# Gate matrices of a 16384-expert layer: outer products on TensorE for three token blocks, or indirect accumulating DMA into DRAM tables for two of them

## The chip, the cores and the metric

The kernel runs on one core of one Trainium2 chip. The metric is the device time of one execution in microseconds (us), less is better. Of the kernel before three timed runs are shown and one profiled execution. TensorE (PE in the profile) multiplies; VectorE (DVE) and ScalarE (ACT) do elementwise work; GpSimd (POOL) here mostly issues DMAs whose addresses come from a table of indices; SyncE (SP) issues nearly all other DMAs.

## What is computed

Two blocks of a network run one behind the other on 512 tokens of width 1024. The change is in the last layer of the second, a mixture of 16384 experts of one row each. Cut to what matters:

```
q = x @ wq                                   # 8 heads, two halves of 128 per head
scores = q . sub_keys                        # 128 scores per half
s_top, i_top = top_k(scores, 16)             # both halves
best_s, best_pos = top_k(all 16*16 sums, 16) # per head
expert = i_top[0]*128 + i_top[1]             # 8*16 = 128 experts per token
gate = softmax(best_s)                       # 128 gates per token
act = gelu(x . u_tab[expert]) * gate
out = sum(act * v_tab[expert])               # then a layer norm
```

## The kernel before

The first 2350 us or so are two layers of feed-forward and token mixing and the second block's token mixing; the change leaves them alone but for one place. What follows is `peer()`.

The 512 tokens are four blocks of 128. **Block 0** takes the reference's way: `chosen()` fetches for each of the 128 expert slots one row of `u_tab`, later one of `v_tab`, for all its 128 tokens by an indirect DMA on POOL's queue (L1737), and DVE multiplies the row (L1721) or adds it up (L1729), three gathers behind the issue; 256 such gathers in all. **Blocks 1 to 3** (384 tokens) are done densely: for each of 128 *columns* j (a column is the 128 experts with first index j) `proj` multiplies all 384 tokens with the column's 128 rows of `u_tab` (24 matmuls, L283, in three groups of eight: high by high, low by high, high by low part), the result goes through Gelu and is multiplied with a matrix of gates that is zero wherever a token did not choose the expert; then the column's rows of `v_tab` are multiplied in (18 matmuls, L1822) and accumulate over all columns. So each column needs a 128 by 384 slab of gates, `G[:, :, j]`.

`route()` finds experts and gates. It is a generator, and each `next()` is a *step*. In four *quads* (four score matrices each, after four units of `wq`) DVE takes the top 16 of each score matrix and of the sums; `resolve` turns positions into indices and softmaxes the gates. Then for six half blocks of 64 tokens (`BLOCKS`) it builds the gate slab: four tokens a step get two one-hot matrices on DVE (`o1` L1679, `o2` L1681), the second scaled by the gate on ACT (`og` L1683), four outer products on TensorE (`gp` L1690), and a copy out on ACT (`st` L1691). A finished half block is written to a DRAM tensor `G` ("gates", L1704); the last stays in SBUF.

The columns pass in three stages.

- **Kept stage.** While routing is unfinished, a column's activation (`hg`, L1839) is written to DRAM (`HS`, "acts"). The loop runs `routed(ROUTE_STEPS)` (2.3 steps of routing a column) and `gather(...)` (1.2, later 0.8 gathers a column) beside each column. It takes 92 columns: `kept` is 92.
- **Fused stage.** The other 36 columns need no store: activation (`hs`), gate, `v_tab` matmuls, with 2.6 gathers a column.
- **Tail.** The 92 kept columns are read back (`hs` from `acts`, `gq` from `gates`, L1876 and L1878) and take their `v_tab` matmuls, one gather a column. The layer norms of the four blocks end the program.

Each weight unit of 512 KB is loaded by SP, its high part is taken on ACT (`wh` L260) and its low part on DVE (`wl` L261); three such pairs and four raw buffers exist. A scheduler orders the instructions of each engine; each engine then runs its own list strictly in that order.

The loop of the kept stage reads:

```
        while not over or kept % 2:
            g = self.t32("hg")[:, GT:]
            activations(kept, g)
            nc.scalar.dma_start(HS[kept], g)
            over = over or routed(ROUTE_STEPS)
            gather(ROW_STEPS[self.known == P])
            kept += 1
```

Of the kernel before, what the change touches and what calls it, by code (L numbers as in the profile page):

```python
# [19 lines left out]
P = 128  # L20
S = 512
# [16 lines left out]

GT = 128
BT = 64  # L40
BLOCKS = [(t, a, a + BT) for t in range(NT) for a in range(0, P, BT) if t * P + a >= GT]

# [4 lines left out]

ROUTE_STEPS = 2.3
ROW_STEPS = (1.2, 0.8, 2.6, 1.0)

# [143 lines left out]
class Net:  # L194
    def __init__(self, tc, A, es):
# [8 lines left out]
        self.phase = es.enter_context(ExitStack())  # L204
        self.evn = 0

        c = self.const
# [320 lines left out]
    def ada_steps(self, l, n):  # L528
# [16 lines left out]
        if kind == 2 and i != 1:  # L545
            nc.vector.tensor_scalar(m, m, 0.5, None, op0=OP.mult)
        yield

    def fill(self, n):
# [1048 lines left out]
    def route(self, X, G, begun):  # L1598
# [3 lines left out]
        best, pos, itop, numbers, iis = {}, {}, {}, {}, {0: self.ii0}  # L1602
        for quad in range(4):
            keys = self.blk(name="keys")
            nc.sync.dma_start(keys, self.A["keys"][:, quad * 4:(quad + 1) * 4].rearrange("p a b -> p (a b)"))
# [6 lines left out]
            for t in range(NT):  # L1612
# [27 lines left out]
                if t == 0:  # L1640
# [6 lines left out]
                    nc.vector.tensor_copy(self.experts[:, q], e)  # L1647
                    self.known += 32
                elif t == BLOCKS[0][0] and quad == 3:
                    iis[t] = self.blk(name="ii")  # L1650
                    yield from self.resolve(best[t], pos[t], itop[t], iis[t], 0, 8)
        for n, (t, a, b) in enumerate(BLOCKS):
            for v in (t, BLOCKS[n + 1][0] if n + 1 < len(BLOCKS) else t):
# [46 lines left out]
            if n == len(BLOCKS) - 1:  # L1700
                self.last_gates = st
            else:
                for q in range(4):
                    nc.sync.dma_start(G[:, n, q * 32:(q + 1) * 32], st[:, q * 32:(q + 1) * 32])  # L1704
                yield
# [40 lines left out]
    def peer(self, out, begun):  # L1746
# [5 lines left out]
        self.pools(blocks, 22, {"A": 3, "S": 1, "T": 4})  # L1752
        n, last, early = S - GT, len(BLOCKS) - 1, GT // P
        G = self.dram.tile([P, last, NE, BT], F32, name="gates")
        HS = self.dram.tile([NE, P, n], F32, name="acts")
# [5 lines left out]
        ln = cst[:, 384:400].rearrange("p (a b) -> p a b", a=2)  # L1761
        nc.gpsimd.dma_start(ln, A["ln"])
        c0 = stage.tile([P, S], F32, name="c0", tag="c0")
        self.ii0, self.gates0, self.experts = c0[:, :256], c0[:, 256:384], c0[:, 384:].bitcast(I32)
# [27 lines left out]

        def routed(steps):
            nonlocal pace
            pace += steps
            while pace >= 1.0:
                pace -= 1.0
                with self.tc.issue_after(self.latest):
                    if next(work, self) is self:
                        return True  # L1800
            return False
# [27 lines left out]

        def gates(tile, j):  # L1830

            g4 = tile.rearrange("p (b i t) -> p b i t", i=2, t=BT)
            nc.sync.dma_start(g4[:, :last], G[:, :, j:j + 2])
            nc.scalar.activation(g4[:, last], self.last_gates[:, j:j + 2], AF.Copy)
            return g4

# [4 lines left out]
        kept, over = 0, False  # L1841
        while not over or kept % 2:
            g = self.t32("hg")[:, GT:]
            activations(kept, g)
            nc.scalar.dma_start(HS[kept], g)
            over = over or routed(ROUTE_STEPS)
            gather(ROW_STEPS[self.known == P])
            kept += 1
        self.kept = kept
        acc += [self.bank("acc", t) for t in "TTTTSA"]  # L1850
        fused, g4 = [], None
        for j in range(kept, NE):
            if j % 2 == 0:
                g4 = gates(stage.tile([P, 2 * n], F32, name="gs", tag="gs"), j)
            hs = self.blk(name="hs")[:, :n]
            activations(j, hs)
            nc.vector.tensor_mul(hs.rearrange("p (b t) -> p b t", t=BT), hs.rearrange("p (b t) -> p b t", t=BT),
                                 g4[:, :, j % 2])
            hi, lo = (v[:, :n] for v in self.new_pair())
            self.split(hs, hi, lo)  # L1860
            fused.append((*self.unit(A["pv"][:, j]), hi, lo))
            gather(ROW_STEPS[2])
            if len(fused) > 1:
                both(fused.pop(0))
# [8 lines left out]
        def fetch(j):  # L1873
            if j < kept:
                hs, g = self.blk(name="hs")[:, :n], self.blk(name="gq")[:, :n]
                nc.sync.dma_start(hs, HS[j])  # L1876
                g3 = g.rearrange("p (b t) -> p b t", t=BT)
                nc.sync.dma_start(g3[:, :last], G[:, :, j])  # L1878
                nc.scalar.activation(g3[:, last], self.last_gates[:, j], AF.Copy)
                coming.append((hs, g))  # L1880
# [44 lines left out]
        for j in range(kept - ENDS):  # L1925
            both(weighted(j) if j else first)
            if not self.gathered:
                gather(ROW_STEPS[3])
                if self.gathered:
# [12 lines left out]
def program(tc, A, out):  # L1942
    with ExitStack() as es:
# [21 lines left out]
        for l in range(DEPTH):  # L1965
            begun = net.ffn(l, 0, begun, lambda: to_mix(l))
            begun = net.mix(l, begun, lambda: to_ffn(l, 1))
            if l + 1 < DEPTH:
                net.side = side(l + 1, (1, 0, 2, 3, 4, 5, 6, 7, 8))
            begun = net.ffn(l, 1, begun, lambda: to_ffn(l + 1, 0) if l + 1 < DEPTH else to_second())  # L1970
        net.peer(out, net.mix2(begun))
# [17 lines left out]
```

## Time and profile before

| what | value |
|---|---|
| median of three timed runs | 3681.9 us (3677.95 to 3684.1) |
| profiled execution, its own time | 3671.99 us |
| its span | 3670.2 us |
| mean granted TensorE clock | 0.988 |
| columns kept / fused | 92 / 36 |

The span is the time from the first to the last instruction of the profiled execution. TensorE is busy for 97% of it, so a stage is best read by how many matmuls it runs and how long it lasts.

### The profile page before, as it was taken

The page shows a single profiled execution, that of the slowest core. Times are in us where ns is not written, and L with a number is a line of the kernel's source. Part 1 is how long each engine was busy: PE and PEld are TensorE (multiplying, and loading weights), DVE is VectorE, ACT ScalarE, POOL GpSimd, SP SyncE. Part 2 cuts the span into 40 slices and gives each one's busy share as a digit, 9 for nine tenths or more (in the row PEclk, how much of TensorE's full clock was granted, in tenths as well). Part 3 has the DMA queues.
Part 4 walks back from the last instruction along what each step waited for, and adds up shares of the span by engine and source line. Part 5 has one row for each costly group of instructions (what it writes and reads, how often), then busy time and mean ns, then how long its engine had stood idle before and what let it go on. Part 6 is the DMA issues. An engine that isn't in the chain of part 4 may idle for free. (4 is left out here: it accounts for less than half of the span.)

```text
span 3670.2 us, 49271 instructions
## 1 busy us (share of the span) xinstructions
PE 3554.5 (97%) x18265; PEld 3019.0 (82%) x18265; DVE 2394.7 (65%) x4791; ACT 1562.9 (43%) x2769; POOL 369.2 (10%) x358
## 2 busy tenths in 40 slices
PE   7999999999999999999999999899899999999998
PEld 6888876788888888767888887788899999988786
DVE  6555687665563334776533386699877667778787
ACT  4332366433233323465432263433667753334333
POOL 0000100000000001000000000021221134432220
PEclk9999999999999999999999999999999999999999
DMA  7666320266653333401333322265686879999995
GB/s 249 190 186 198 115 94 18 64 202 193 201 178 109 94 95 105 133 24 31 91 98 93 97 79 68 84 202 195 206 289 235 296 262 308 313 327 346 336 341 183
DMA packets 259665, 635.72 MB, mean 173 GB/s; under 512 B 82336, under 2 KB 117584, under 8 KB 256864
## 3 DMA queue, kind: packets, MB, share of 16 engines
q1 hardware_dynamic: 206368, 473.96, 40.1%
q0 software_dynamic: 39808, 140.52, 11.2%
q10 hardware_dynamic: 13248, 18.09, 1.3%
q8 instruction: 143, 2.34, 0.3%
q14 instruction: 98, 0.80, 0.1%
HBM read 591.32 MB, written 41.16 MB: 172 GB/s over the span
## 5 line engine op out<-in xcount | busy, mean ns | idle before, releaser
L260 ACT ACTIVATE wh<-raw 128x1024 fp32r<-128x1024 f32 (+2 forms) x620 | 645.3, 1043 | 1129.3 <-PE proj L283 880.6
L261 DVE TENSOR_TENSOR wl<-raw,wh 128x1024 fp32r<-128x1024 f32 (+2 forms) x620 | 744.1, 1201 | 508.4 <-ACT wh L260 370.1
L283 PE MATMUL proj<-yh,wh 128*128 128x512 f32 (+1 forms) x2744 | 644.7, 375 | 9.1 <-ACT hg L1839 4.2
L283 PE MATMUL proj<-yh,wl 128*128 128x512 f32 (+1 forms) x2744 | 629.1, 371 | 13.6 <-DVE wl L261 13.6
L283 PE MATMUL proj<-yl,wh 128*128 128x512 f32 (+1 forms) x2744 | 628.4, 370 | 0.0
L283 PEld LDWEIGHTS proj<-yh,wl 128*128 128x128 f32 x2744 | 506.4, 189 | 82.8 <-DVE wl L261 15.5
L283 PEld LDWEIGHTS proj<-yh,wh 128*128 128x128 f32 x2744 | 501.1, 189 | 85.0 <-ACT hg L1839 5.7
L283 PEld LDWEIGHTS proj<-yl,wh 128*128 128x128 f32 x2744 | 505.4, 189 | 67.5
L535 DVE SCALAR_TENSOR_TENSOR scr<-raw,cact 128x1024 bf16<-128x1024 f32 x128 | 156.7, 1224 | 136.3 <-DMA raw<-in_wada 136.0
L1822 PE MATMUL acc<-wl,yh 128*128 128x512 f32 x756 | 236.2, 394 | 2.7 <-DVE wl L261 2.6
L1822 PE MATMUL acc<-wh,yh 128*128 128x512 f32 x756 | 235.0, 392 | 3.6 <-ACT yh L266 2.1
L1822 PE MATMUL acc<-wh,yl 128*128 128x512 f32 x756 | 234.3, 391 | 0.3 <-DVE yl L267 0.3
L1737 POOL DMA_INDIRECT row<-in_purows,c x128 | 156.5, 1223 | 537.9 <-DVE row L1721 261.6
L667 DVE TENSOR_TENSOR ga<-sg,proj 128x512 f32<-128x512 f32 x88 | 60.5, 687 | 225.7 <-PE proj L283 223.2
L1737 POOL DMA_INDIRECT row<-in_pv,c x128 | 165.2, 1291 | 392.6 <-DVE vacc L1729 275.8
L272 PE MATMUL proj<-yl,wh 128*128 128x256 f32 (+1 forms) x552 | 177.0, 330 | 10.6 <-DVE yl L394 7.0
L273 PE MATMUL proj<-yh,wl 128*128 128x256 f32 (+1 forms) x552 | 174.6, 324 | 2.2 <-DVE wl L261 2.2
L1822 PEld LDWEIGHTS acc<-wl,yh 128*128 128x128 f32 x756 | 141.1, 188 | 38.4 <-DVE wl L261 9.5
L271 PE MATMUL proj<-yh,wh 128*128 128x256 f32 (+1 forms) x552 | 164.8, 328 | 7.8 <-ACT yh L640 6.3
L1822 PEld LDWEIGHTS acc<-wh,yh 128*128 128x128 f32 x756 | 142.1, 189 | 32.0 <-ACT yh L266 2.5
L1822 PEld LDWEIGHTS acc<-wh,yl 128*128 128x128 f32 x756 | 142.5, 189 | 31.4 <-DVE yl L267 1.0
L1729 DVE SCALAR_TENSOR_TENSOR vacc<-row,act,vacc 128x1024 f32<-128x1024 f32 x127 | 162.5, 1280 | 0.6
(465 smaller groups left out, 5166.7 us busy)
## 6 DMA issues: line engine op xcount, KB each, us to landing
raw<-in_wada SPq DMA_DIRECT2D x144, 512.0 KB
raw<-in_pu SPq DMA_DIRECT2D x128, 512.0 KB
raw<-in_pv SPq DMA_DIRECT2D x128, 512.0 KB
raw<-in_wg SPq DMA_DIRECT2D x84, 512.0 KB
raw<-in_wu SPq DMA_DIRECT2D x84, 512.0 KB
raw<-in_wd SPq DMA_DIRECT2D x64, 512.0 KB
gates<-st SPq DMA_DIRECT2D x20, 1024.0 KB
acts<-hg ACTq DMA_DIRECT2D x92, 192.0 KB
```

Source lines behind the costliest of these rows:

```text
L260: nc.scalar.activation(h[:, :n], raw[:, :n], AF.Copy)
L261: self.latest = nc.vector.tensor_sub(l[:, :n], raw[:, :n], h[:, :n].bitcast(F32)).ins
L271: mm(out, lhsT=lh, rhs=rh, start=start, stop=False)
L272: mm(out, lhsT=lh, rhs=rl, start=False, stop=False)
L273: mm(out, lhsT=ll, rhs=rh, start=False, stop=stop)
L283: self.nc.tensor.matmul(ps, lhsT=w[:, k * P:(k + 1) * P], rhs=X[c + k][part], start=c + k + i == 0, stop=i == 2 and c + k == nk - 1)
L535: nc.vector.scalar_tensor_tensor(scr, raw, 1.0, self.cact, op0=OP.mult, op1=OP.mult, accum_out=self.mod[:, l, j:j + 1])
L667: nc.vector.tensor_mul(a, sg, p[1])
L1729: nc.vector.scalar_tensor_tensor(acc, row, a, acc, op0=OP.mult, op1=OP.add)
L1737: nc.gpsimd.indirect_dma_start(out=row, out_offset=None, in_=tables[kind], in_offset=bass.IndirectOffsetOnAxis(ap=self.experts[:GT, s:s + ...
L1822: nc.tensor.matmul(acc[q], lhsT=a[:, t * P:(t + 1) * P], rhs=half(w, m), start=q not in started, stop=end and i == 2)
```

## The change

Gates of token blocks 1 and 2 are no longer built by outer products. Two DRAM tables of 16384 by 128 numbers (8 MB each, `table1`, `table2`) are set to zero during the last feed-forward of the first network, by 32 DMAs of 512 KB on POOL's queue. In each quad `resolve` now also runs for blocks 1 and 2 (two heads at a time, as for block 0), an index `expert*128 + token` is computed, and `spread_gates` issues for each of 128 slots and both tables one indirect DMA with add: 128 gates, one from each partition, four bytes each, to 128 places of the table (L1837). Only block 3 keeps its outer products (2 half blocks in place of 6). Routing now takes 2.3 steps a column in the first quad, 1.0 in the others and 1.8 behind them; 1.3 slots a column are spread; gathers go at 0.9 a column in the kept stage. The stage also lasts until all slots are issued: the built program keeps 110 columns (110 DMAs to `acts`) and fuses 18. A column's gates are now read by three DMAs (two tables and `G`) in place of one.

```
+TABLES = (1, 2)
-BLOCKS = [(t, a, a + BT) for t in range(NT) for a in range(0, P, BT) if t * P + a >= GT]
+BLOCKS = [(NT - 1, a, a + BT) for a in range(0, P, BT)]
-ROUTE_STEPS = 2.3
-ROW_STEPS = (1.2, 0.8, 2.6, 1.0)
+ROUTE_STEPS = (2.3, 1.0, 1.8)
+TABLE_STEPS = 1.3
+ROW_STEPS = (0.9, 2.6, 1.0)
...
+    def clear_tables(self):
+        nc = self.nc
+        for T in self.tables:
+            for q in range(NE // 8):
+                if q % 4 == 0:
+                    z = self.t32("zero")
+                    nc.gpsimd.memset(z, 0.0)
+                out = T[q * 8 * P * P:(q + 1) * 8 * P * P].rearrange("(p a c) o -> p a (c o)", p=P, a=2)
+                with self.tc.issue_after(self.latest):
+                    nc.gpsimd.dma_start(out, z[:, None, :].to_broadcast([P, 2, S]))
+                yield
...
+                elif t in TABLES:
+                    ii, q, n = self.blk(name="ii"), quad * 32, TABLES.index(t)
+                    yield from self.resolve(best[t], pos[t], itop[t], ii, quad * 2, 2)
+                    e, idx = self.sm(32, "enum"), self.idx[:, n * P + q:n * P + q + 32]
+                    nc.vector.scalar_tensor_tensor(e, ii[:, P + q:P + q + 32], float(NE), ii[:, q:q + 32],
+                                                   op0=OP.mult, op1=OP.add)
+                    nc.vector.tensor_scalar(e, e, float(P), self.pid, op0=OP.mult, op1=OP.add)
+                    nc.vector.tensor_copy(idx, e)
+                    self.ready[n] += [(idx[:, i:i + 1], best[t][:, q + i:q + i + 1]) for i in range(32)]
...
+        def spread_gates(columns):
+            nonlocal share
+            share = min(share + columns, 2.0)
+            while share >= 1.0 and all(self.ready):
+                share -= 1.0
+                for T, r in zip(self.tables, self.ready):
+                    idx, g = r.pop(0)
+                    with self.tc.issue_after(self.latest):
+                        nc.gpsimd.indirect_dma_start(out=T, out_offset=bass.IndirectOffsetOnAxis(ap=idx, axis=0), in_=g,
+                                                     in_offset=None, compute_op=OP.add)
...
-        def gates(tile, j):
-            g4 = tile.rearrange("p (b i t) -> p b i t", i=2, t=BT)
-            nc.sync.dma_start(g4[:, :last], G[:, :, j:j + 2])
...
+        def gates(tile, j, m):
+            g3 = tile.rearrange("p (i t) -> p i t", i=m)
+            for i, T in enumerate(self.tables):
+                nc.sync.dma_start(g3[:, :, i * P:(i + 1) * P],
+                                  T[j * P * P:(j + m) * P * P].rearrange("(i p t) o -> p i (t o)", p=P, t=P))
+            nc.sync.dma_start(g3[:, :, n - 2 * BT:n - BT], G[:, j:j + m])
+            nc.scalar.activation(g3[:, :, n - BT:], self.last_gates[:, j:j + m], AF.Copy)
...
-        while not over or kept % 2:
+        while not over or kept % 2 or self.ready[0]:
...
-            over = over or routed(ROUTE_STEPS)
-            gather(ROW_STEPS[self.known == P])
+            over = over or routed()
+            spread_gates(TABLE_STEPS)
+            gather(ROW_STEPS[0])
...
+            else:
+                net.side = net.clear_tables()
```

On POOL's queue, in the kept stage, there stood only gathers of block 0 (`row` from `in_purows`), each waiting for DVE to free a row buffer:

```order
L1737 DMA row<-in_purows,c_19132 128x1024 [waits DMASW4_49,DVE_49]
L1737 DMA row<-in_purows,c_19132 128x1024 [waits DMASW5_49,DVE_49]
L1737 DMA row<-in_purows,c_19132 128x1024 [waits DMASW6_49,DVE_49]
L1737 DMA row<-in_purows,c_19132 128x1024 [waits DMASW7_49,DVE_49]
L1737 DMA row<-in_purows,c_19132 128x1024 [waits DMASW0_49,DVE_49]
```

In the same stage of the changed kernel the two tables (`table_72` and `table_73`) alternate between the gathers; DMASWn are the semaphores of POOL's own earlier DMAs, used in turn:

```order
L1837 DMA table_73<-x_91,idx 2097152x1 [waits DMASW6_49,DVE_49,Activation_49]
L1837 DMA table_72<-x_90,idx 2097152x1 [waits DMASW5_49]
L1837 DMA table_73<-x_91,idx 2097152x1 [waits DMASW6_49]
L1837 DMA table_72<-x_90,idx 2097152x1 [waits DMASW7_49]
L1837 DMA table_73<-x_91,idx 2097152x1 [waits DMASW0_49]
L1837 DMA table_72<-x_90,idx 2097152x1 [waits DMASW1_49]
L1837 DMA table_73<-x_91,idx 2097152x1 [waits DMASW2_49]
L1766 DMA row<-in_purows,c_19184 128x1024 [waits DVE_49]
L1837 DMA table_72<-x_90,idx 2097152x1 [waits DMASW3_49]
```

Each of these waits names the semaphore of the previous DMA to the same table, two places up, so a scatter is issued only when the one before it to its table has landed. Between the first and the last scatter stand 256 scatters and 73 gathers; in 54 places the next scatter goes to the same table as the last. The first of them stand ahead of the gather whose row DVE takes at column 15, the last behind that of column 95.

On TensorE, in the later part of the kept stage, outer products (`gp`) stood between the columns' matmuls:

```order
L283 MATMUL proj<-yh,wl 128x384 x8
L283 MATMUL proj<-yl,wh 128x384 x8
L283 MATMUL proj<-yh,wh 128x384 x2
L1690 MATMUL gp<-og,o_23913 128x128 x3
L283 MATMUL proj<-yh,wh 128x384
L1690 MATMUL gp<-og,o_23913 128x128
L1690 MATMUL gp<-og,o_23922 128x128
```

In the changed kernel most of the stage holds columns and now and then the score matmuls of a quad (`sc`):

```order
L288 MATMUL proj<-yh,wh 128x384 x8
L288 MATMUL proj<-yl,wh 128x384 x8
L288 MATMUL proj<-yh,wl 128x384 x8
L1639 MATMUL sc<-keys,x_93 128x128
L1639 MATMUL sc<-keys,x_94 128x128
L1639 MATMUL sc<-keys,x_95 128x128
L1639 MATMUL sc<-keys,x_96 128x128
```

The outer products went from 384 to 128 and now stand only near the end of the stage.

On SP's queue, in the tail, a column had three DMAs:

```order
L1876 DMA hs<-acts 128x384
L1878 DMA gq<-gates 128x5x64
L257 DMA raw<-in_pv 128x1024
L1876 DMA hs<-acts 128x384
L1878 DMA gq<-gates 128x5x64
```

Now it has five:

```order
L1926 DMA hs<-acts 128x384
L1881 DMA gq<-table_72 128x128
L1881 DMA gq<-table_73 128x128
L1883 DMA gq<-gates 128x64
L262 DMA raw<-in_pv 128x1024
```

The bytes of a column's gates are the same; they come from three tensors.

## Rows read from the trace of the kernel before

**Rows 1.** The page, its part 1: busy time by engine.
```profile
PE 3554.5 (97%) x18265; PEld 3019.0 (82%) x18265; DVE 2394.7 (65%) x4791; ACT 1562.9 (43%) x2769; POOL 369.2 (10%) x358
```

**Rows 2.** Writers of the activations: ns min/median/max of one, first and last start.
```profile
L1839 ACT ACTIVATE hg<-proj x92: 463/490/500, 2365.8 to 2966.1; 128x384 f32<-128x384 f32 x92
...
L1839 ACT ACTIVATE hs<-proj x36: 473/492/492, 2970.3 to 3256.9; 128x384 f32<-128x384 f32 x36
```

**Rows 3.** Busy times of the engines in four stretches, with granted clock and DMA.
```profile
core 0: us, PE busy (x) PEld busy (x) DVE busy (x) ACT busy (x) POOL busy (x), PEclk, DMA share, GB/s
1600.00:2100.00 500.00, 490.32 (x2456) 397.34 (x2456) 232.43 (x444) 194.74 (x356) 2.08 (x4) 0.99 0.25 75
...
2445.00:2608.00 163.00, 146.38 (x736) 134.96 (x735) 150.96 (x676) 54.05 (x71) 22.39 (x20) 0.92 0.53 172
2608.00:2966.00 358.00, 345.34 (x2225) 341.55 (x2224) 267.57 (x440) 263.70 (x612) 74.18 (x55) 1.00 0.76 264
...
3257.00:3630.00 373.00, 368.25 (x1591) 298.86 (x1590) 298.55 (x400) 147.14 (x278) 88.68 (x85) 0.99 0.99 333
```

**Rows 4.** Timeline of TensorE: start and length in us, then the instructions.
```profile
2705.28 1.63 PE L283 MATMUL proj<-yh,wh 128*128 128x384 f32 x8
...
2709.52 1.95 PE L1690 MATMUL gp<-og,o 128*128 128x128 f32 x16
2711.23 0.94 PE L283 MATMUL proj<-yh,wh 128*128 128x384 f32 x4
```

**Rows 5.** Timeline of TensorE earlier in the kept stage.
```profile
2457.49 0.84 PE L283 MATMUL proj<-yl,wh 128*128 128x512 f32 x3
2462.61 2.93 PE L283 MATMUL proj<-yh,wl 128*128 128x384 f32 x8 [4.28 <-DVE wl L261]
...
2471.51 1.98 PE L283 MATMUL proj<-yh,wh 128*128 128x512 f32 x8
...
2476.95 1.98 PE L283 MATMUL proj<-yh,wh 128*128 128x512 f32 x8
...
2482.39 0.83 PE L1620 MATMUL sc<-keys,x 128*128 128x128 f32 x6
```

**Rows 6.** Groups by line and shape, 2366 to 2966: busy us, mean ns, idle before.
```profile
L261 DVE TENSOR_TENSOR wl<-raw,wh 128x1024 fp32r<-128x1024 f32 x104 | 126.7, 1222 | 76.8 <-ACT wh L260 69.4 <-PE proj L283 6.6 <-issue 0.8
...
L1690 PE MATMUL gp<-og,o 128*128 128x128 f32 x768 | 100.8, 279 | 9.4 <-ACT og L1683 8.7 <-ACT st L1691 0.8
...
L1679 DVE TENSOR_TENSOR o<-pcst,tr 128x512 f32<-128x512 f32 x96 | 65.5, 687 | 11.8 <-PE gp L1690 11.7
...
L1729 DVE SCALAR_TENSOR_TENSOR vacc<-row,act,vacc 128x1024 f32<-128x1024 f32 x29 | 37.1, 1279 | 0.1
L1681 DVE TENSOR_TENSOR o<-iota,tr 128x512 bf16<-128x512 bf16 x96 | 37.0, 421 | 9.8 <-issue 5.5 <-DMA acts<-hg 4.3
```

**Rows 7.** Timeline of POOL where gathers stand back to back.
```profile
2388.93 1.01 POOL L1737 DMA_INDIRECT row<-in_purows,c  x1 [61.56 <-DVE pcst L1551]
2390.24 0.99 POOL L1737 DMA_INDIRECT row<-in_purows,c  x1 [0.30 <-issue]
2391.54 0.93 POOL L1737 DMA_INDIRECT row<-in_purows,c  x1 [0.30 <-issue]
```

**Rows 8.** Timeline at the program's start: a DMA's issue and its first user.
```profile
0.76 0.39 SPq L509 DMA_DIRECT2D x<-in_x  x1
...
1.28 0.72 POOL L210 DMA_DIRECT2D ident<-in_ident  x1 [0.82 <-POOLq L1980]
...
3.57 0.63 ACT L605 ACTIVATE sq<-x 128x512 f32<-128x512 f32 x1 [1.53 <-DMA x<-in_x]
...
6.07 0.23 DVE L214 CAST identb<-ident 128x128 bf16<-128x128 f32 x1 [4.68 <-DMA ident<-in_ident]
```

**Rows 9.** The tail's gate reads by tile: ns of one issue on SP.
```profile
L1878 SPq DMA_DIRECT2D gq<-gates x92: 523/524/721, 3259.1 to 3607.6; - x92
```

**Rows 10.** Groups by line and shape, 3257 to 3630: who waits for the gates.
```profile
L1891 DVE TENSOR_TENSOR hs<-hs,gq 128x384 f32<-128x384 f32 x92 | 50.7, 557 | 69.6 <-DMA gq<-gates 67.5 <-ACT gq L1879 1.9
```

More of the change, by code (lines that the diff above doesn't have):

```diff
@@ L205, in __init__ @@
         self.evn = 0
+        self.tables = [self.dram.tile([NE * NE * P, 1], F32, name=f"table{t}") for t in TABLES]
         c = self.const
@@ L1603, in route @@
         for quad in range(4):
+            self.part = min(quad, 1)
             keys = self.blk(name="keys")
@@ L1651, in route @@
                     yield from self.resolve(best[t], pos[t], itop[t], iis[t], 0, 8)
+        self.part = 2
         for n, (t, a, b) in enumerate(BLOCKS):
@@ L1703, in route @@
                 for q in range(4):
-                    nc.sync.dma_start(G[:, n, q * 32:(q + 1) * 32], st[:, q * 32:(q + 1) * 32])
+                    nc.sync.dma_start(G[:, q * 32:(q + 1) * 32], st[:, q * 32:(q + 1) * 32])
                 yield
@@ L1752, in peer @@
         self.pools(blocks, 22, {"A": 3, "S": 1, "T": 4})
-        n, last, early = S - GT, len(BLOCKS) - 1, GT // P
-        G = self.dram.tile([P, last, NE, BT], F32, name="gates")
+        n, early = S - GT, GT // P
+        G = self.dram.tile([P, NE, BT], F32, name="gates")
         HS = self.dram.tile([NE, P, n], F32, name="acts")
@@ L1762, in peer @@
         nc.gpsimd.dma_start(ln, A["ln"])
+        self.pid = cst[:, 400:401]
+        src = A["iota"]
+        nc.gpsimd.dma_start(self.pid, bass.AP(tensor=src.tensor, offset=src.offset, ap=[[1, P], [1, 1]]))
+        self.idx = stage.tile([P, 2 * P], I32, name="idx", tag="idx")
+        self.ready, self.part = [[] for _ in TABLES], 0
         c0 = stage.tile([P, S], F32, name="c0", tag="c0")
@@ L1791, in gather, with routed @@
                     credit = credit - 1.0 if next(rows, False) else 0.0
-        def routed(steps):
+        share = 0.0
+        def spread_gates(columns):
[8 more added lines that the diff above has]
+                                                     in_offset=None, compute_op=OP.add)
+        def routed():
             nonlocal pace
-            pace += steps
+            pace += ROUTE_STEPS[self.part]
             while pace >= 1.0:
@@ L1828, in both @@
                 second(*args, end, t)
-        def gates(tile, j):
-            g4 = tile.rearrange("p (b i t) -> p b i t", i=2, t=BT)
-            nc.sync.dma_start(g4[:, :last], G[:, :, j:j + 2])
-            nc.scalar.activation(g4[:, last], self.last_gates[:, j:j + 2], AF.Copy)
-            return g4
+        def gates(tile, j, m):
[5 more added lines that the diff above has]
+            nc.scalar.activation(g3[:, :, n - BT:], self.last_gates[:, j:j + m], AF.Copy)
+            return g3
         def activations(j, g):
@@ L1850, in peer @@
         acc += [self.bank("acc", t) for t in "TTTTSA"]
-        fused, g4 = [], None
+        fused, g3 = [], None
         for j in range(kept, NE):
             if j % 2 == 0:
-                g4 = gates(stage.tile([P, 2 * n], F32, name="gs", tag="gs"), j)
+                g3 = gates(stage.tile([P, 2 * n], F32, name="gs", tag="gs"), j, 2)
             hs = self.blk(name="hs")[:, :n]
             activations(j, hs)
-            nc.vector.tensor_mul(hs.rearrange("p (b t) -> p b t", t=BT), hs.rearrange("p (b t) -> p b t", t=BT),
-                                 g4[:, :, j % 2])
+            nc.vector.tensor_mul(hs, hs, g3[:, j % 2])
             hi, lo = (v[:, :n] for v in self.new_pair())
@@ L1861, in peer @@
             fused.append((*self.unit(A["pv"][:, j]), hi, lo))
-            gather(ROW_STEPS[2])
+            gather(ROW_STEPS[1])
             if len(fused) > 1:
@@ L1876, in fetch @@
                 nc.sync.dma_start(hs, HS[j])
-                g3 = g.rearrange("p (b t) -> p b t", t=BT)
-                nc.sync.dma_start(g3[:, :last], G[:, :, j])
-                nc.scalar.activation(g3[:, last], self.last_gates[:, j], AF.Copy)
+                gates(g, j, 1)
                 coming.append((hs, g))
@@ L1927, in peer @@
             if not self.gathered:
-                gather(ROW_STEPS[3])
+                gather(ROW_STEPS[2])
                 if self.gathered:
```

## The prediction

> **What bounds the kernel now.** I read the page's busy shares first: TensorE is busy for 97% of the span, DVE for 65%, POOL for 10% [rows 1]. A total like that says who has the most to do, not where time is lost, so I next split the part that the change touches into its stages by the writers of the activations [rows 2]: kept stage 2365.8 to 2966.1 (600 us for 92 columns), fused stage to 3256.9 (35 intervals, 8.19 us a column), then the tail, 373 us for 92 columns, 4.05 each [rows 3].
>
> What should the kept stage take if TensorE never waited? A column's 24 matmuls run from 2705.28 to 2709.52, 4.24 us; 16 rows of outer products, which are eight matmuls, take the 1.71 us behind them, 0.107 a row [rows 4]. A `wq` unit of 24 matmuls takes 5.44 us, a row of score matmuls some 0.1 [rows 5]. So 92 x 4.24 = 390, thirteen `wq` units (sixteen less the three done ahead) 71, 768 rows of outer products 82, 128 rows of scores 13: together 556. The stage lasts 600, so 44 us are lost. The stretches say where [rows 3]: of 2445 to 2608 TensorE is busy 146 of 163 us at a granted clock of 0.92, while DVE is busy 151: DVE is the limit there (routing at 2.3 steps a column). The 17 idle us and 0.08 x 146 = 12 us of clock make 29. From 2608 to 2966 it is 13 more of 358, at full clock. One such stall shows both halves of the price: TensorE waits 4.28 us for a low part from DVE, and the eight 384-column matmuls that follow take 2.93 us, where eight take 1.4 elsewhere, at the lower level of the clock [rows 5].
>
> **The change, part by part.**
>
> *Outer products.* 512 of the 768 rows go: 512 x 0.107 = 55 us of TensorE, on the path, since TensorE has no slack there. On DVE 64 steps of 687 + 421 ns go, 71 us [rows 6].
>
> *Routing paced anew.* In quads two to four DVE now has one step a column, not 2.3. From 2445 to 2608 it was busy 151 us for some 18 columns: 26 low parts at 1.22 us are 32, some 20 gathers' rows at 1.28 are 26 [rows 3, 6], so 41 steps took 93, 2.3 us a step. In a column of the changed kernel that gives 2.3 + 1.22 + 0.9 x 1.28 + a share of `wq` 0.2 = 4.9 us of DVE against 4.24 of TensorE plus 12 units of 5.44 over some 72 columns, 5.1. DVE just fits. The two added `resolve`s a quad are steps like the others, so they are in the 2.3. I take a remaining loss of 13 us, as in the second stretch of before: 31 us gained. If DVE does not fit, this gain goes (bound: 0 to 44).
>
> *Columns moved.* Kept 110 x 4.24 + 71 + 27 + 13 = 577, and 13 lost: 590, so 10 less than now. Eighteen fused columns fewer: -18 x 8.19 = -147. Eighteen in the tail more: +18 x 4.05 = +73. Sum: **-84 us**, if nothing new binds. This is the 55 and some 30 of stalls, so the moves themselves are neutral.
>
> *Scatters.* This is the new cost. 256 indirect DMAs enter POOL's queue, each held until the previous one to its table has landed. Behind a waiting scatter stand the gathers; for those waits DVE (it takes a row three gathers later), behind which stand low parts, and for them TensorE. SP is tied too: the first read of a table waits for its last scatter, and weight loads stand behind it. By the order, 54 scatters follow one to their own table and the other 202 make 101 alternating pairs, so the chain has 155 landings in a row. Its room is TensorE's time between the rows that DVE takes at columns 10 and 96: 86 x 4.24 + 12 x 5.44 + 15 of scores and outer products = 445 us.
>
> How long is one landing? The trace has no accumulating DMA. From below: issues alone. Gathers follow each other on POOL after 1.24 to 1.31 us, 0.93 to 1.01 busy and 0.30 between [rows 7]; (256 + 73) x 1.25 = 411 us, which fits. From above: the first load on POOL's queue is used 4.8 us after its issue [rows 8]; 155 x 4.8 = 744. Between: the first load of SP is used at 3.57, 2.4 us after its 0.39 us issue [rows 8]; with a gather's 0.93 in front that is 3.35. That load has 256 KB, 0.8 us at the tail's 333 GB/s [rows 3], a scatter 512 bytes: 2.55. The add has to read its target first, and the engines are 0.76 busy. I take **2.8**, near the lower end. A gather in front on the same queue can add from nothing (its issue lies in the wait) to its 512 KB, 1.6 us at that rate; I take 0.8 for each of 73, 58 us. Chain: 155 x 2.8 + 58 = 492; it overruns its room by **47 us**.
>
> The Trainium skill ("DMA: Bandwidth & Descriptors", Anatomy of one DMA, SWDGE path) fits about 2.0 us plus bytes over 436 GB/s to a DMA of this queue, and adds that the completion "can cause a surprisingly long delay especially when the write target is HBM". By the figure alone (an estimate) 155 x 2.0 = 310 us would hide under the issues, and the whole 84 us would come; by the warning, which no run here shows, the chain would be longer than mine. The trace's 2.4 us behind the issue lies a little over the figure.
>
> *Clearing the tables.* 32 DMAs of 512 KB, one a weight unit of 24 full matmuls, so within some 180 us of the last feed-forward: 93 GB/s on top of 75, where the tail moves 333 [rows 3]. POOL is idle there (2.08 of 500). Nil; if it collided, at most 16.8 MB at 333 GB/s, 50 us.
>
> *Gate reads.* SP issues three of about 0.52 us a column in place of one [rows 9]; with the two other loads under 2.5 of 4.05 us. The bytes stay. DVE already waits 67.5 us for `gq` in the tail [rows 10], and TensorE is busy 368 of 373 all the same: nil, bound below.
>
> **Sum.** The profiled execution took 3672.0 (1.8 around its span). 3672 - 84 + 47 = 3635; the runs' median lies 10 above that execution, so **3645 us**, -1.0%.
>
> **Rivals.** A measurement of this kernel tells about 0.2%, 7 us, from no change.
>
> - *The chain hides.* It needs a chain under 445: landings of 2.5 with no delay by gathers. Then -84: 3598. For it: POOL is busy 10%; against: the stage's DMA share of 0.76, in which a gather's data delay what follows. Chance 0.16. The Trainium skill's figure above would lead here.
> - *The chain decides* (other side). Equal to before at a chain of 445 + 84 = 529, so at a landing of 3.04 us with the same 58. At 3.6 it is 616: 3682 - 84 + 171 = 3769. The place is POOL's queue between columns 15 and 95, the sign DVE idle before L1721 and L1729 until a row lands, and TensorE behind it, at times at the lower clock. For it: 3.35 and 4.8 in the rows; that 2.8 is barely under the border is the weak point of my sum. Chance 0.33.
> - *The tail pays.* At a DMA share of 0.99, if three short reads cost a column 0.4 us more, 110 columns cost 44 and nearly nothing is left: 3689. For it: the 67.5 us; against: TensorE's 368 of 373. Chance 0.06.
>
> **Chances and range.** Forecast 0.45, its own range 3605 to 3672 (landings of 2.55 to 3.0). With the hidden chain that makes faster 0.57; 0.04 of the forecast, 0.03 of the tail and 0.03 of the chain near its border make same 0.10; slower 0.33. The range reaches from 3592, just under the hidden chain, to 3755, a landing of 3.5; outside it lie 0.15 above and 0.04 below.
>
> **What would show it.** 128 outer products and 110 columns kept. POOL's scatters following each other by table at 2.8 us; the kept stage near 637 us; TensorE's time between stalls unchanged, 4.24 us a column; the DVE-bound stretch gone, the granted clock there near 1. Fused stage 18 x 8.2, tail 110 x 4.05, POOL's clears without effect on the feed-forward. Wrong it is if a scatter lands well after 3 us, or if an indirect DMA with add takes POOL longer to issue than a gather.

## The result, and the profile after

| what | before | after |
|---|---|---|
| median of the timed runs | 3679.9 us (3675.2 to 3684.1, 4 runs) | 3917.9 us (3917.1 to 3921.1, 4 runs) |
| ratio | 1 | 1.065 [1.063, 1.067] |
| span of the profiled execution | 3670.2 us | 3915.8 us |
| mean granted TensorE clock | 0.988 | 0.959 |

The change makes the kernel 6.5% slower; 3645 us was forecast. The page, part 1, after; against [rows 1], TensorE falls from 97% to 91% while its busy time stays, for 518 fewer matmuls, and POOL rises from 369 to 798 us:

```profile
PE 3549.3 (91%) x17747; PEld 3000.5 (77%) x17747; DVE 2345.6 (60%) x4779; ACT 1467.7 (37%) x2476; POOL 797.9 (20%) x655
```

The writers of the activations, and the reads of stored ones in the tail, by tile (ns min/median/max of one, first and last start), against [rows 2]:

```profile
L1889 ACT ACTIVATE hg<-proj x110: 468/492/499, 2365.7 to 3263.3; 128x384 f32<-128x384 f32 x110
...
L1926 SPq DMA_DIRECT2D hs<-acts x110: 319/377/676, 3406.2 to 3846.1; - x110
L1939 DVE TENSOR_TENSOR hs<-hs,gq x110: 551/558/597, 3413.8 to 3852.8; 128x384 f32<-128x384 f32 x110
L1889 ACT ACTIVATE hs<-proj x18: 492/492/493, 3267.4 to 3404.5; 128x384 f32<-128x384 f32 x18
```

By stages (first to last `hg`, on to the last `hs`, on to the end of the span): kept 600 to 898 us (+298), fused 291 to 141 (-150), the rest 413 to 511 (+98). Sum +246, the difference of the spans. The kept stage alone turned the sign. Its busy times in stretches, with those of the tail behind them:

```profile
core 0: us, PE busy (x) PEld busy (x) DVE busy (x) ACT busy (x) POOL busy (x), PEclk, DMA share, GB/s
2366.00:2410.00 44.00, 44.00 (x261) 43.19 (x260) 38.44 (x180) 20.28 (x27) 8.88 (x9) 1.00 0.69 219
2410.00:3160.00 750.00, 500.73 (x2475) 473.93 (x2474) 392.78 (x1263) 209.57 (x318) 514.97 (x331) 0.83 0.58 141
3160.00:3264.00 104.00, 95.98 (x584) 95.04 (x583) 56.77 (x84) 57.75 (x122) 22.77 (x22) 0.95 0.82 281
3406.00:3870.00 464.00, 444.61 (x1915) 356.09 (x1914) 356.41 (x484) 176.93 (x334) 109.67 (x106) 1.00 0.96 326
```

Ahead of the first scatter and behind the last one TensorE is nearly full. Between them it idles 249 us of 750 and runs at a granted clock of 0.83; nobody is full there, DMA stands at 0.58, and POOL, busy 515 us, looks idle a third of the time. It isn't. The scatters' line, then POOL's groups of the stretch (busy us, mean ns, idle before it):

```profile
L1837 POOL DMA_INDIRECT table<-x,idx x256: 1532/1556/2620, 2409.8 to 3160.2; - x128
...
  DMA table<-x,idx: 163.0, 104
  issue: 49.8, 149
...
DMA to landing us min/median/max: 2.9/3.4/7.7
```

```profile
L1837 POOL DMA_INDIRECT table<-x,idx x256 | 430.1, 1680 | 217.5 <-DMA table<-x,idx 163.0 <-issue 49.8 <-DVE pcst L1571 2.6
L1766 POOL DMA_INDIRECT row<-in_purows,c x41 | 49.0, 1196 | 12.5 <-issue 9.1 <-DVE pcst L1572 0.6 <-DVE pcst L1571 0.6
L1766 POOL DMA_INDIRECT row<-in_pv,c x32 | 35.6, 1112 | 9.7 <-issue 7.9 <-DVE at L1591 0.3 <-DVE pcst L1568 0.3
```

430.1 + 217.5 for the scatters and 106.8 for the 73 gathers make 754 us, the whole stretch. What shows that POOL's queue is full is what its idle time ends at: a landing of an earlier scatter (163) or the gap between two issues (67), and DVE for less than 10 us. An issue takes 1.56 us (mean 1.68) and 0.30 pass before the next; 104 times it waits for a landing on top. Its timeline:

```profile
2724.43 1.65 POOL L1837 DMA_INDIRECT table<-x,idx  x1 [0.30 <-issue]
2728.98 2.15 POOL L1837 DMA_INDIRECT table<-x,idx  x1 [2.90 <-DMA table<-x,idx]
2731.44 1.07 POOL L1766 DMA_INDIRECT row<-in_pv,c  x1 [0.31 <-issue]
2732.81 2.01 POOL L1837 DMA_INDIRECT table<-x,idx  x1 [0.30 <-issue]
2735.12 1.55 POOL L1837 DMA_INDIRECT table<-x,idx  x1 [0.30 <-issue]
2736.98 0.99 POOL L1766 DMA_INDIRECT row<-in_pv,c  x1 [0.30 <-issue]
```

Who waits, in the same 750 us (total, times, longest), and behind it how soon a gather lands after its issue begins, in the whole run:

```profile
PE proj L288 <- DVE wl L266: 189.1, 31, 29.2
DVE row L1750 <- DMA row<-in_purows,c: 181.9, 30, 32.1
POOL table L1837 <- DMA table<-x,idx: 163.0, 104, 5.8
DVE vacc L1758 <- DMA row<-in_pv,c: 132.4, 20, 39.1
```

```profile
DMA to landing us min/median/max: 4.2/5.8/15.0
```

The path is this: a gather stands behind scatters on POOL, DVE waits 314 us for rows, low parts stand behind those waits, TensorE waits for low parts. DVE's waits of up to 39 us are longer than any landing of a gather that the trace gives (15.0), so the longest of them are waits for a late issue, not for slow data alone. In [rows 7] a gather followed a gather after 1.3 us; here the scheduler's order has up to 22 scatters ahead of one.

### The profile page after: what moved, and what is told of

Same layout as the page of the kernel before. It is cut to its first block, busy times and chain, and to the rows that moved or that the text cites. A ratio compares the mean times of both kernels' runs of the same rounds, so it can differ in the third digit from the quotient of the medians.

```text
span 3915.8 us, 48637 instructions
## 1 busy us (share of the span) xinstructions
PE 3549.3 (91%) x17747; PEld 3000.5 (77%) x17747; DVE 2345.6 (60%) x4779; ACT 1467.7 (37%) x2476; POOL 797.9 (20%) x655
## 4 chain that ended last, share of the span: by engine, by line
PE 64%; DMA 12%; DVE 9%; POOL 7%; issue 5%; ACT 2%; SPq 1%; DVEq 0%; ACTq 0%; POOLq 0%
PE proj L288 42%; PE acc L1869 6%; POOL table L1837 6%; DMA table<-x,idx 5%; DMA gq<-gates 3%; DVE wl L266 2%; PE proj L277 2%; PE proj L276 2%; PE proj L278 2%; PE o L1109 1%; PE tp L887 1%; POOL row L1766 1%; PE sc L827 1%; DMA row<-in_purows,c 1%; DVE ch L1361 1%
## 5 line engine op out<-in xcount | busy, mean ns | idle before, releaser
L288 PE MATMUL proj<-yh,wl 128*128 128x512 f32 (+1 forms) x2744 | 652.4, 381 | 189.1 <-DVE wl L266 189.1
L288 PEld LDWEIGHTS proj<-yh,wl 128*128 128x128 f32 x2744 | 522.1, 196 | 266.7 <-DVE wl L266 199.8
L288 PE MATMUL proj<-yh,wh 128*128 128x512 f32 (+1 forms) x2744 | 657.4, 382 | 23.7 <-ACT hg L1889 20.1
L288 PEld LDWEIGHTS proj<-yh,wh 128*128 128x128 f32 x2744 | 521.8, 196 | 98.7 <-ACT hg L1889 22.0
L1837 POOL DMA_INDIRECT table<-x,idx x256 | 430.1, 1680 | 217.5 <-DMA table<-x,idx 163.0
L1750 DVE SCALAR_TENSOR_TENSOR row<-row,cact 128x1024 f32<-128x1024 f32 x128 | 155.5, 1221 | 182.6 <-DMA row<-in_purows,c 182.6
L1766 POOL DMA_INDIRECT row<-in_purows,c x128 | 146.3, 1143 | 335.7 <-DVE row L1750 200.5
L1766 POOL DMA_INDIRECT row<-in_pv,c x128 | 146.5, 1144 | 273.1 <-DVE vacc L1758 185.7
```

Source lines behind the costliest of these rows:

```text
L288: self.nc.tensor.matmul(ps, lhsT=w[:, k * P:(k + 1) * P], rhs=X[c + k][part], start=c + k + i == 0, stop=i == 2 and c + k == nk - 1)
L1750: nc.vector.scalar_tensor_tensor(row, row, 1.0, XN, op0=OP.mult, op1=OP.mult, accum_out=a)
L1766: nc.gpsimd.indirect_dma_start(out=row, out_offset=None, in_=tables[kind], in_offset=bass.IndirectOffsetOnAxis(ap=self.experts[:GT, s:s + ...
L1837: nc.gpsimd.indirect_dma_start(out=T, out_offset=bass.IndirectOffsetOnAxis(ap=idx, axis=0), in_=g, in_offset=None, compute_op=OP.add)
```

## The experiments

Theory: the chain of scatters on POOL is longer than TensorE's work beside it, and the excess is the loss. Rivals: the scatters' 32768 four-byte targets (both tables together; two expectations below count twice that) slow the loads wherever they stand; or the new pacing, the added `resolve`s or the gate reads cost it. 17 kernels ran.

**Without scatters, and pacing alone.** Two runs take the change apart.

```
e1_no_scatters: spread_gates() pops idx, g and issues nothing
e3_pacing_only, on the kernel before:
-ROUTE_STEPS = 2.3                  +ROUTE_STEPS = (2.3, 1.3, 2.3)   # first quad, quads 2-4, behind
```

> The changed kernel without its 256 scatters; everything else, the clearing and reading of the tables too, stays. It leaves out the gates of token blocks 1 and 2. Theory: the scatters' serial chain on POOL costs all of the loss, so without it what the prediction worked out for the rest should come: kept stage near 590 us, 3590 to 3615 us in all. Rival (added resolves, the new pacing or the three gate reads cost it): the kept stage stays well over 620 us and the time over 3680.

> The kernel before with nothing but routing paced anew: 2.3 steps a column in the first quad, 1.3 in the other three, 2.3 behind them; all three blocks keep their outer products. 110 columns are kept. By the prediction's term for the pacing it gains the stalls of the stretch in which DVE was the limit, some 30 us: 3645 to 3660. Rival (the stalls have another cause, or return where the outer products stand): 3675 to 3690.

Without scatters: **3604.6 us**, 0.981 [0.979, 0.983], kept stage 580 us:

```profile
2366.00:2950.00 584.00, 573.54 (x3332) 559.60 (x3332) 485.88 (x1525) 292.80 (x467) 112.05 (x105) 0.99 0.76 248
```

So clearing, added `resolve`s, pacing and gate reads are not the loss; the scatters cost 317 us of the kept stage. TensorE idles 10 us there, and 257 in the kept stage of the changed kernel (its three rows above). The rest of the 317 goes with the clock: nearly the same matmuls (3320, 3332) take 641 us busy in place of 574, at 0.85 over the stage in place of 0.99. The trace ascribes each of the 257 us to DVE's or ACT's work, 189 of them to low parts.

Pacing alone: **3660.7 us**, 0.997 [0.996, 0.998], the only version that beats both kernels (by 0.3% before) and leaves nothing out. In the stretch where DVE was the limit [rows 3] TensorE idles 6.4 us, where it idled 17, at 0.99:

```profile
2445.00:2608.00 163.00, 156.60 (x851) 147.11 (x850) 141.90 (x595) 62.76 (x82) 31.43 (x29) 0.99 0.70 225
2608.00:2966.00 358.00, 349.70 (x2223) 346.68 (x2222) 286.53 (x545) 246.31 (x541) 80.84 (x57) 1.00 0.76 263
```

**No gathers beside the scatters.** This takes DVE off POOL's queue and puts contention to the test.

```
e8_no_gathers_beside:        -ROW_STEPS = (0.9, 2.6, 1.0)  +ROW_STEPS = (0.0, 2.6, 1.9)
e12_reads_held, with e8's:   in gates(): with self.tc.issue_after(<the last weight load>): nc.sync.dma_start(... T ...)
e17_four_tables_no_gathers, with e12's: a block's scatters go to two tables in turn, one of them is read
e19_fast_scatters_alone, with e17's:    -in_offset=None, compute_op=OP.add)  +in_offset=None)
```

> The changed kernel without gathers in the kept stage: they come at 2.6 a column in the fused stage and 1.9 in the tail. So DVE waits for nothing that stands behind scatters on POOL. Theory (the loss reaches DVE and TensorE by the gathers alone): the kept stage is that without scatters, some 590 us, TensorE full; the scatters end near 2409 + 607 = 3016 us, the fused stage waits some 60 us for them, and the tail's added 0.9 gathers a column cost some 40: 3680 to 3720 us. Rival (the scatters' 32768 descriptors per table take DMA engines from the weight loads): the kept stage stays over 700 us and the time over 3850.

> The kernel without gathers in the kept stage, and SP's first reads of the tables held behind the weight load of column 109. In the run without gathers they stood behind load 88, and load 89 waited 221 us for the scatters to end. Theory (nothing is lost beside the scatters, only where an engine's queue waits for their end): the kept stage ends near 2956 us, the scatters near 3065, so the wait shrinks from 221 to some 110 us: 3770 to 3790 us. Rival (the scatters take longer once loads run beside them all the way, or slow the loads): 3850 or more.

> No gathers in the kept stage, table reads held on SP, and four tables (half of the gates of blocks 1 and 2 are left out). Theory: 256 issues of 1.85 to 1.98 us are 474 to 507 us, from 2410 to some 2900, before the kept stage ends at 2957: no wait for them is left, so of the 3821 with two tables the wait of some 150 us goes: 3660 to 3680 us, the tail with 1.9 gathers a column included. If scatters take their 685 us whatever they wait for: 3820.

> No gathers in the kept stage, table reads held on SP, four tables, and scatters that write instead of adding (half of the gates of blocks 1 and 2 are left out). A scatter then takes POOL 1.27 us, 256 of them 325. Theory: they end some 100 us before the kept stage's end, the 45 us wait of the run with the add goes: 3640 to 3650 us, TensorE full until then. Rival (a scatter every 1.27 us slows TensorE, as the pauses in the short chain's run could mean): TensorE is busy under 95% of 2411 to 2700 or at a lower clock, and the time is 3665 or more.

Measured: **3887.0**, **3821.3**, **3689.5**, **3658.1 us** (the last 0.996 [0.994, 0.997]). All four came out above the range of their theory, the last three by 31, 10 and 8 us; the first missed by far, and showed a second path. Its stretches, then SP's queue and TensorE (start and length, instructions, idle before):

```profile
2411.00:2800.00 389.00, 386.60 (x2159) 374.18 (x2160) 286.49 (x1061) 173.12 (x224) 233.25 (x138) 0.99 0.66 158
2800.00:3020.00 220.00, 17.91 (x118) 17.59 (x116) 5.59 (x9) 9.18 (x23) 159.78 (x104) 0.55 0.22 3
```

```profile
2742.84 46.98 SPq L262 DMA_DIRECT2D raw<-in_pu  x12
3027.17 0.39 SPq L1881 DMA_DIRECT2D gs<-table  x1
```

```profile
3034.31 2.07 PE L1719 MATMUL gp<-og,o 128*128 128x128 f32 x8 [216.40 <-ACT og L1712]
```

For 389 us TensorE is full beside the scatters. Then SP stops: in its order the first read of a table, used at column 110, stands behind the load of column 88, so load 89 waits until the last scatter to that table has landed, and ACT, which takes its high part, waits with it:

```profile
ACT wh L265 <- DMA raw<-in_pu: 238.1, 2, 221.3
```

Held back to column 110 (e12), TensorE's longest wait begins there and shrinks from 216 to 161 us; with four tables (e17), where the scatters' waits for landings fall from 219 to 76 us, to 35; with a shorter issue too (e19) it is gone. The same 489 us without scatters (e1), and with one every 2.2 us (e17):

```profile
2411.00:2900.00 489.00, 478.54 (x2764) 465.59 (x2763) 416.75 (x1305) 243.52 (x385) 92.68 (x87) 0.99 0.76 251
```

```profile
2411.00:2900.00 489.00, 485.44 (x2809) 472.74 (x2809) 337.65 (x1151) 248.93 (x397) 367.27 (x219) 0.99 0.71 164
```

TensorE does 2764 matmuls without scatters and 2809 beside them (gathers are missing there). So contention falls as far as scatters and loads go: scatters that nothing waits for cost TensorE nothing here. Scatters and gathers together are another matter, below (e15). All four pay 52 to 56 us behind the fused stage (566 to 570 us, 514 without scatters), for the some 99 gathers more that the tail takes at a DMA share of 1.0 and more.

**What makes the chain long.**

```
e2_four_tables:  a block's scatters go to two tables in turn, one of them is read
e9_plain_scatter: -in_offset=None, compute_op=OP.add)  +in_offset=None)
e5_pool_order:   with self.tc.issue_after(<POOL's last indirect DMA>): around each scatter and gather
e16_four_tables_order: e5 and e2;  e15_short_chain: e5, e2 and e9
```

> The changed kernel with two tables more: each block's scatters alternate between two tables, so that a scatter waits for the landing of the one four places up. Only one table of each block is read, so half of the gates of blocks 1 and 2 are left out. The number of scatters, their descriptors and bytes stay. Theory (a landing in series behind each issue): the 163 us of waits for landings go, the chain is 256 x 1.98 + 73 x 1.3 = 602 us of issues in place of 750; 3720 to 3775 us. Rival 1 (65536 accumulating four-byte writes slow the DMA engines and the loads): as the changed kernel, near 3918. Rival 2 (issues alone were never the limit, only the landings): near 3600.

> The changed kernel with scatters that write instead of adding: where a token has one expert twice, one of its gates is lost. If the add makes POOL's issue long, it falls from 1.56 us to that of a gather, 1.0, the chain gets 143 us shorter, and the time is near 3775. If 128 targets of four bytes make it long, it stays 1.56 and the time stays near 3918, unless landings get shorter without the read of the target: by up to 163 us of waits.

> The changed kernel with POOL's indirect DMAs held to the order in which the program writes them. In the changed kernel the scheduler lets a quad's scatters stand in bunches (14, 8, 17, 22 in a row) ahead of a gather whose row DVE needs soon; here two to four scatters stand between gathers, up to column 106. Theory (total time on POOL against the columns it lies beside): 256 x 1.98 + some 92 x 1.4 = 636 us against a room of 96 columns, 500; 136 too long, 3605 + 136 = 3740 us; up to 3800 if landings with a gather's data in front are waited for. Rival (only the sum of issues and landings counts, the order of POOL doesn't): 3900 or more.

> POOL in written order and four tables, with the add (half of the gates of blocks 1 and 2 are left out). Theory: landings drop out of the chain, issues stay: 256 x 1.97 + 97 x 1.35 = 635 us beside 520: some 115 too long, 3605 + 115 = 3720 us, of the 3820 in written order alone. If landings in pairs cost nothing there already: 3820.

> POOL in written order, four tables, and scatters that write instead of adding (half of the gates of blocks 1 and 2 are left out): as many scatters, descriptors, bytes and gathers as in the changed kernel, but an issue of 0.97 us and no table used again for four scatters. Theory (the loss is the length of POOL's chain over the columns beside it): 256 x 1.27 + 97 x 1.35 = 456 us beside 104 columns, some 520: hidden, so the time is that without scatters, 3600 to 3630 us. If the separate gains only add up (34 by four tables, 73 by plain writes, 98 by order, from 3918): 3713.

Measured: **3884.2**, **3845.0**, **3820.5**, **3757.4**, **3689.4 us**, all above what their theory gave, by 109 (e2), 70, 20, 37 and 59 us (e15). The scatters' line without the add, in e9:

```profile
L1837 POOL DMA_INDIRECT table<-x,idx x256: 952/971/2993, 2415.5 to 3086.0; - x128
...
DMA to landing us min/median/max: 2.1/3.1/6.4
```

The add makes an issue 1.56 us instead of 0.97, and the landing, counted from the start of the issue, 3.4 instead of 3.1; so without the add a scatter lands no sooner behind its issue, and of 131 us of issues that go, 47 come back as waits for landings (163 to 210). Four tables in the scheduler's order gain little: there a gather stands behind up to 38 scatters in a row, and DVE waits up to 58 us for one. Held to written order (e5) the chain is as long as before, 741 us, but lies beside 102 columns, not 84; order and tables together (e16) gain 160. The next table has the runs that scatter both blocks beside 110 kept columns; the chain runs from the first scatter's start to the last's, "beside" is the number of columns whose activation ends in between, the room what these columns take in the run without scatters:

| run | chain | beside | room | excess | kept stage over 580 |
|---|---|---|---|---|---|
| changed kernel | 750 | 84 | 446 | 304 | 317 |
| e2, four tables | 680 | 77 | 407 | 273 | 280 |
| e9, plain writes | 670 | 84 | 446 | 225 | 238 |
| e8, no gathers | 662 | 83 | 440 | 222 | 226 |
| e5, written order | 741 | 102 | 540 | 202 | 216 |
| e12, no gathers, reads held | 684 | 100 | 531 | 153 | 158 |
| e16, order, four tables | 678 | 101 | 535 | 143 | 152 |
| e15, and plain writes | 598 | 98 | 523 | 75 | 79 |
| e17, no gathers, four tables | 563 | 100 | 531 | 32 | 32 |
| e19, and plain writes | 466 | 89 | 472 | -5 | -7 |

By itself the agreement only says that all the loss lies between the first scatter and the last. That POOL makes it follows from what POOL's idle time ends at in the changed kernel, from TensorE's waits there, and from the last two rows, where the loss goes as the chain gets shorter. One row doesn't fit: in e15 POOL is busy 423 of 664 us and its landings are waited for some 7 us in all, and yet 79 us are lost. TensorE's waits there, from 2366 to 3030:

```profile
PE proj L289 <- issue: 28.2, 56, 1.4
PE proj L289 <- ACT hg L1894: 8.7, 1, 8.7
PE gp L1720 <- issue: 4.9, 9, 1.0
```

It pauses in 56 places for nothing that the trace shows, and the same matmuls take 617 us busy at a clock of 0.94, 574 without scatters at 0.99. e19 issues the same scatters without gathers and shows none of it, and the changed kernel has no such pause. What plain scatters and gathers do together stays open.

**One table, and fewer gathers.** Attempts to make the idea pay.

```
e4_one_table: -TABLES = (1, 2)  +TABLES = (1,)   -BLOCKS: block 3  +BLOCKS: blocks 2 and 3
              +ROUTE_STEPS = (2.3, 1.2, 1.4)  +TABLE_STEPS = 1.1
e6_one_table_order: e4 with e5's order
e10_one_table_few: e6 with e12's reads  +ROW_STEPS = (0.45, 2.6, 1.6)  +TABLE_STEPS = 1.15
e13_two_tables_few: e5 with e12's reads +ROW_STEPS = (0.45, 2.6, 1.6)  +TABLE_STEPS = 1.15
```

> One table: block 1 by 128 scatters, blocks 2 and 3 by outer products; 1.1 scatters, 1.2 (quads two to four) and 1.4 (behind) routing steps a column; 126 columns are kept. Theory: every scatter waits for the landing of the one before it, 128 x 3.7 = 474 us, which fits beside 126 columns of some 4.9 us (617) if the gathers are issued inside the landings; then 27 us of outer products and some 30 of stalls are gained: 3620 to 3650. If each gather adds its 1.3 us (113 of them), the chain is 620 and just fits: up to 3690. Rival (each scatter slows the loads by 320 / 256 = 1.25 us wherever it stands): 3682 - 57 + 160 = 3785.

> One table as before (128 scatters, 126 columns kept), with POOL's indirect DMAs in written order: scatters and gathers in turn, over some 118 columns instead of 64. Theory: the chain is 128 x 4.4 = 563 us, as with one table in the scheduler's order, but its room grows from 64 columns (some 350 us) to 118 (some 600): it fits, 3625 to 3660 us. If each gather's data delay the next landing further, up to 3710. Rival (each scatter slows everything by 1.5 us or more wherever it stands): 3850 again.

> One table, POOL's indirect DMAs in written order, 1.15 scatters and 0.45 gathers a column (not 0.9), the other gathers at 1.6 a column in the tail, table reads held on SP. Theory: a scatter costs 3.7 us, and about 0.8 more for each gather in front: 128 x 4.0 = 510 us beside some 110 columns of 4.9 us (540): hidden. Kept stage 126 x 4.24 + 71 + 40 = 651, tail as with one table in order (594 us) plus up to 20 for DVE: 3630 to 3660 us. If a scatter's landing stays near 5 us (as with gathers in turn), 3690 to 3720.

> Both tables, POOL in written order, 1.15 pairs of scatters and 0.45 gathers a column, the other gathers at 1.6 a column in the tail, table reads held on SP; 120 columns kept. Theory (POOL's time against the columns): a column costs POOL 1.15 x 2 x 1.98 + 0.45 x 1.35 = 5.2 us, TensorE 5.1: just hidden, if a table's next scatter, 3.96 us behind the last, needn't wait for its landing (3.4): 3620 to 3660 us. If landings are waited for (4.0 median with gathers' data in front), some 0.3 us a pair, 40 us more: up to 3700. If POOL's 741 us of chain stay whatever the order: 3820.

Measured: **3855.0**, **3725.0**, **3740.8**, **3801.0 us**; all slower than before (1.014 to 1.049), all over the range that their theory gave. With one table a scatter waits for the one just ahead: 4.4 us each from 2411 to 2974, beside 64 columns in the scheduler's order (the program spreads the 128 scatters over some 116). Written order gives them their columns back and 130 us. Fewer gathers, with the reads held (e10), shorten the kept stage by another 32 us (749 to 717) and cost 52 in the tail. With both tables (e13) the chain is still 701 us, beside 110 columns.

**Finer pacing.**

```
e11_pacing_finer:         e3 with +ROUTE_STEPS = (2.0, 1.2, 2.1)  +ROW_STEPS = (0.8, 0.8, 2.6, 1.1)
e18_pacing_gathers_early: e3 with +ROW_STEPS = (1.2, 1.2, 2.6, 0.7)
```

> Only pacing, further: the kernel before with 2.0, 1.2 and 2.1 routing steps and 0.8 gathers a column in the kept stage (122 columns kept), 1.1 gathers in the tail. Pacing alone gained 14 us and left some 16 us of waits for low parts between 2450 and 2950. If DVE's load a column (1.2 x 2.3 + 1.22 + 0.8 x 1.28 = 5.0 us) below TensorE's 5.1 is what counts, most of these go: 3640 to 3655 us. If what is left comes of bursts inside a step, no change: 3660.

> Pacing only, and gathers earlier: 2.3, 1.3, 2.3 routing steps as in the first run with pacing alone, 1.2 gathers a column in the whole kept stage and 0.7 in the tail. In four runs a gather more in the tail cost some 0.6 to 0.7 us, where DMA is busy all the time; where outer products are built DVE is busy 73% and DMA 78%. 30 gathers moved there save up to 20 us if they cost nothing there: 3640 to 3655 us. If they bring stalls there: 3660 to 3670.

Measured: **3681.1** (1.002 of before) and **3734.6 us**, both worse than 3660.7. In the second, 33 us are lost in the kept stage and 46 behind the fused one, although DMA and DVE have less to do there: TensorE waits 43.1 us for low parts in the tail, with one gather a column 6.8. Why the tail's order gets worse with fewer gathers wasn't tried.

## Why the prediction was wrong

*The scatters, the step that failed.* The sum put their chain at 492 us against a room of 445. The room was right: the 84 columns beside the chain take 446 (86 were counted, at a little less each). The chain is 750. Two prices in it were too low. The landing, taken as 2.8, is 3.4; and the issue was left at a gather's 0.93 to 1.01 us [rows 7], as "issues alone ... 411 us, which fits", and is 1.56, mean 1.68, with 0.30 behind it. So a pair to two tables takes 2 x 1.98 = 4.0 us by issues alone, no longer hidden under one landing. The 750 are 430 of issues, 50 of gaps, 163 of waits for landings and 107 of gathers (58 in the sum). The landing alone doesn't explain it: the prediction's own chain with 3.4 is 155 x 3.4 + 58 = 585. With 305 instead of 47 of excess, the prediction's own sum gives 3672 - 84 + 305 = 3893, and its +10 for the median 3903; 3918 came, and the 15 left are what the base of -84 was too good by (below). It named both ways to be wrong ("a scatter lands well after 3 us", "an indirect DMA with add takes POOL longer to issue than a gather"), but priced only the first.

The Trainium skill ("DMA: Bandwidth & Descriptors", Anatomy of one DMA, SWDGE path) counts descriptor generation as a "small, variable" part of a fixed 2.0 us. This trace differs: 1.56 us of the 3.4 are issue, and issues with their gaps alone (256 x 1.98 = 507 us) exceed the room. Its warning of a long completion points the right way: landings here have 2.9 at least, 3.4 in the middle and 7.7 at most. The prediction's 2.4 us, set beside that figure, was of a load on SP's queue; on POOL's own the first load was used 4.8 us after its issue.

*The rival that came true.* "The chain decides": place (POOL's queue) and sign (DVE idle for rows, TensorE behind it, clock 0.83) were as described; its border, a chain of 529, no run tests; its price, 3769 at a landing of 3.6, was 150 short, again for the issue. Chance given: 0.33. "The chain hides" is what e19 shows, at 0.96 us an issue and without gathers beside it; its chain of 466 still holds 126 us of waits for landings.

*Base of -84.* Without scatters 3604.6 against the 3674.6 measured beside it: -70. The kept stage was 580 (590 forecast), the fused 8.06 a column (8.19); what is missing lies in the tail (+101, not +73). Pacing alone brought 14 us, and yet that term was nearly right: 110 columns were kept in 649 us, where 600 and 18 x 4.24 make 676, so the stalls gave 27 of the 31. But the moves weren't neutral: they cost 12 in that run, as the tail took 85 us for its 18 columns, not 73.

*Tail.* The reads of `acts` are 4.04 us apart; 4.05 was forecast, but the kernel before has 3.83 by the same measure (its `gates` reads in [rows 9]; 4.05 there was with the ends). The tail as a whole grew by 98, not 73. The three gate reads in place of one are what is left for 13 of that: 511 us behind the fused stage, 498 with pacing alone, as many columns and 111 gathers in place of 112. How they cost it isn't shown (DVE waits some 85 us for `gq` in both). Forecast: nil, with 44 as a rival.

*Clearing the tables.* The first `hg` starts at 2365.7, before at 2365.8: nil, as forecast.

*Queues passed.* SP's waiting table read was named, not priced. In the changed kernel it stands behind load 92 of 128, and the one wait for it that shows (ACT's) is 22.0 us; without gathers it alone held TensorE for 216.

## What to carry to other kernels

Before many small DMAs go on a queue, price one by three numbers, issue, gap and landing, and multiply; a queue whose engine shows 69% busy can be full. Then look who else stands in that queue and in what order the scheduler puts them: one late gather, or one early read on another queue, hands the whole excess to the engine that bounds the kernel. Test the price with the extra work left out and, separately, with nobody waiting for it: the one gives the loss, the other tells a queue from contention.

## What the runs showed of the hardware

An indirect DMA with add takes POOL 1.56 us to issue, one that writes the same 128 elements 0.97, a gather of 128 rows of 4 KB 1.01. An adding scatter of 512 bytes lands 3.4 us after its issue begins (2.9 to 7.7; 3.1 in the middle without gathers, e8), a writing one after 3.1 (2.1 to 6.4; 3.5 in e19), a gather of 512 KB after 4.7 (its `u_tab` rows, 2411 to 2974). Beside 256 adding scatters in 563 us, 32768 targets of four bytes, with loads but no gathers, TensorE was busy 485 of 489 us (e17). In stretches where waits broke TensorE's work up, its granted clock was 0.83 over 750 us, and 0.55 over 220 us in which it was busy 18.
